# Two of seven Strassen products of an FFN tile done ahead for one chunk, in place of classically multiplied tiles

## The chip, the cores and the metric

The kernel runs on one core of one Trainium2 chip. A core has five engines that run side by side, each through its own instruction queue in order: TensorE (PE in the profile) multiplies, VectorE (DVE), ScalarE (ACT) and GpSimd (POOL) work on tiles elementwise, SyncE (SP) issues the DMAs. The metric is the device time of one execution in microseconds; lower is better. Before the change it is 2269.41 us, the median of three runs (2268.31 to 2272.55).

## The reference, cut to what matters

Two layer pairs over 1024 tokens of width 1024 in float32. Each pair is a mixer and a gated feed-forward network (FFN) with a causal depthwise convolution of width 3; the second mixer is itself a convolution of width 31. The change lies in the FFN's up-projection, which both pairs have:

```
def conv_ffn(h, w_up, dw_w, dw_b, w_down):          # h: 1024 x 1024, w_up: 1024 x 5632
    hh = causal_dwconv(h @ w_up, dw_w, dw_b)         # width 3 along the tokens
    a, gate = jnp.split(hh, 2, axis=-1)              # 2816 value and 2816 gate columns
    return (a * jax.nn.silu(gate)) @ w_down
x = x + conv_ffn(rms_norm(x, norm_ffn_g[l]), ...)
```

## The kernel before

Activations are held transposed (model dimension on the partitions). The tokens are two chunks of 512 (`CH`), the hidden width 22 tiles (`HT`) of 128 columns; hidden tile j has 128 gate columns and 128 value columns. Every float32 product is done in three fp32r passes (high x high, high x low, low x high), so each operand is kept as a high and a low part: ACT casts the high part (L143), DVE or GpSimd subtracts it for the low part (L147). One matmul is a 128x128 weight block by 128x512.

A **classical** hidden tile (`head_steps`) takes 48 matmuls a chunk and convolves straight out of PSUM on DVE (L585, L588). It needs no other chunk, so it can run while the second chunk is not ready: it fills PE beside the norm of the second chunk and the steps that build the combinations. Layer 0 has `PRE0` = 3 such tiles, layer 1 `PRE1` = 8.

All other tiles are **pair** tiles (`pair_steps`). The 2x2 block product {gate, value columns} x {two halves of the model dimension} x {two chunks} is done by seven products of 12 matmuls (84 in place of 96). Products 1 to 4 use the chunks' own activations (`hT[0]`, `hT[1]`), products 5 to 7 combinations of them (`T[1]`, `T[2]`, `T[3]`, the tiles t12 and t3), which `combos` builds once per layer (L636 to L639, transposed at L647, split at L649 and L650). The weights' sides are a1 = g1, a2 = g2, a4 = v2, a7 = g1 - v1, and a5, a6, a3, sums built one on the other at L700, L703 and L705. PSUM banks A and C accumulate: product 1, then 6, 7 and 4 into A, 5 and 3 into C, 2 into a bank of its own; between them ACT copies out what an output needs (L715, L718, L721, L732) and DVE adds (L723, L725, L728) into `row` tiles. Each row is then convolved in a two-bank PSUM tile, of which there is one: ACT starts it (L686), DVE adds two taps (L688), ACT takes SiLU of the gate (L730), DVE multiplies (L734).

In layer 1 the down-projection is done by seven products as well, over pairs of hidden tiles j and j + 11; `sums` (L554 to L558, three operations on GpSimd, one on DVE) forms their combinations after the second tile of a pair, called through `settle()` at the start of the next tile. The tile framework puts each engine's instructions in order from the program's order and its own costs; `interleave` mixes two lists of steps. A tile waits for a free buffer of its tag: 8 operand splits `hl`, 4 raw weight tiles, 4 rows, 4 single banks.

The lines that the prediction's steps touch: products L680, operand sums L700 to L705, low parts L147, adds L723 to L728, taps L688, and

```
a5 = part(s, "dve")
nc.vector.tensor_sub(out=s, in0=s, in1=g1)
a6 = part(s, "dve")
nc.gpsimd.tensor_sub(out=s, in0=g2, in1=s)
```

Of the kernel before, what the change touches and what calls it, by code (L numbers as in the profile page):

```python
# [58 lines left out]
def trunk_kernel(ctx: ExitStack, tc: tile.TileContext, x, norm_mix_g, norm_ffn_g, ab_w_in, ab_w_out,  # L59
# [515 lines left out]
    def head_steps(l, c, hT, js):  # L575

        dw, halo, w_up = dws[l], halos[l], ffn_w_up[l]

        def up(ct):
            ps = chan_mm(chan_unit(w_up, ct), hT[c])  # L580
            y = s2([P, CH])
            nc.scalar.activation(out=y, in_=ps, func=AF.Identity, scale=dw[:, 2, ct:ct + 1], bias=dw[:, 3, ct:ct + 1])  # L582
            for k in range(2):
                sh = 2 - k
                nc.vector.scalar_tensor_tensor(out=y[:, sh:], in0=ps[:, :CH - sh], scalar=dw[:, k, ct:ct + 1],  # L585
                                               in1=y[:, sh:], op0=ALU.mult, op1=ALU.add)
                if c > 0:
                    nc.vector.scalar_tensor_tensor(out=y[:, :sh], in0=halo[:, ct, k:2], scalar=dw[:, k, ct:ct + 1],  # L588
                                                   in1=y[:, :sh], op0=ALU.mult, op1=ALU.add)
            if c < NCH - 1:  # L590
                nc.vector.tensor_copy(out=halo[:, ct, :], in_=ps[:, CH - 2:])
            return y

        cur = {}

        def up_g(j):
            cur["g"] = yg = up(HT + j)
            nc.scalar.activation(out=yg, in_=yg, func=AF.Silu)

        def up_a(j):  # L600
            ya = up(j)
            nc.vector.tensor_tensor(out=ya, in0=ya, in1=cur["g"], op=ALU.mult)
            if l == 0:
                store_split(ya, s2([P, CH], F32R), j, slice(c * CH, (c + 1) * CH))
            elif c == 0:
                nc.sync.dma_start(out=phs[:, SLOT[1 + j // HH], j % HH, :], in_=ya)
            elif j < HH:
                cur["v"] = ya
            else:
                jj = j - HH  # L610
                old = s4([P, S])
                nc.sync.dma_start(out=old.rearrange("p (i c) -> p i c", i=2), in_=phs[:, 0:3:2, jj, :])
                sums(jj, old[:, :CH], cur["v"], old[:, CH:], ya)
                nc.sync.dma_start(out=phs[:, SLOT[4], jj, :], in_=ya)
                nc.sync.dma_start(out=phs[:, SLOT[7], jj, :], in_=cur["v"])

        return [f for j in js for f in (lambda j=j: up_g(j), lambda j=j: up_a(j))]
# [553 lines left out]
```

## Time and profile before

| | us |
|---|---|
| median of 3 runs | 2269.41 (2268.31 to 2272.55) |
| the profiled execution itself | 2265.38 |
| its span, first to last instruction | 2263.6 |
| PE busy | 2138.7 (94%) |
| DVE busy | 1481.1 (65%) |
| ACT busy | 1092.8 (48%) |
| POOL busy | 905.1 (40%) |
| mean granted TensorE clock | 0.972 of full speed |

In time, layer 0's classical tiles and combinations lie about 505 to 597 us, its pair tiles 597 to 958. The convolution mixer's end with layer 1's first classical tiles is at 1466 to 1640, the rest of them with norm and combinations at 1640 to 1755, layer 1's pair tiles at 1755 to 2030, its down-projection after that. An engine is listed as busy only while an instruction runs; idle time is listed in front of the instruction that ended it, with the engine and tile that released it.

### The profile page before, as it was taken

How to read it: one execution, taken by the hardware profiler on the slowest of the kernel's cores; microseconds unless marked ns; L12 is line 12 of the kernel's file. 1: busy time of each engine (PE TensorE's matmuls, PEld its weight loads, DVE VectorE, ACT ScalarE, POOL GpSimd, SP SyncE). 2: the span in 40 equal slices, each digit the busy share in tenths (PEclk: the TensorE clock that was granted, in tenths of full speed). 3: DMA queues.
4: the chain of work that ended last, by engine and by line, in shares of the span. 5: the costliest groups of instructions: out<-in, count | busy, mean ns of one | idle time of the engine just before them, and what ended most of it. 6: DMA issues, size and time to landing. Idle time of an engine off the chain costs nothing. (4 is left out here: it accounts for less than half of the span.)

```text
span 2263.6 us, 28251 instructions
## 1 busy us (share of the span) xinstructions
PE 2138.7 (94%) x9846; PEld 1755.1 (78%) x9846; DVE 1481.1 (65%) x2671; ACT 1092.8 (48%) x1899; POOL 905.1 (40%) x772
## 2 busy tenths in 40 slices
PE   8989999898999999999999979989998999999987
PEld 6768777787788888878788868767777888878876
DVE  5456787458666666600399569996576576756686
ACT  4245665244455555522455474555443454544354
POOL 1222010134344443344489827963544455530011
PEclk9999999999999999999999979989989999999999
DMA  6375433466233333588655723432653223238433
GB/s 226 112 244 172 128 124 134 141 231 197 75 112 105 108 107 109 201 305 286 212 168 168 259 60 100 152 100 93 221 165 127 95 91 117 93 132 319 130 98 107
DMA packets 300495, 346.58 MB, mean 153 GB/s; under 512 B 12988, under 2 KB 207296, under 8 KB 299840
## 3 DMA queue, kind: packets, MB, share of 16 engines
q1 hardware_dynamic: 300352, 344.77, 46.3%
q8 instruction: 78, 1.28, 0.2%
q14 instruction: 65, 0.53, 0.1%
HBM read 261.62 MB, written 83.10 MB: 152 GB/s over the span
## 5 line engine op out<-in xcount | busy, mean ns | idle before, releaser
L147 POOL TENSOR_TENSOR hl<-raw,hl 128x512 fp32r<-128x512 f32 x424 | 570.5, 1364 | 605.4 <-ACT hl L143 511.5
L307 PE MATMUL bank<-big,hl 128*128 128x512 f32 x1824 | 427.7, 394 | 4.1 <-ACT big L223 2.4
L270 PE MATMUL bank<-hl,big 128*128 128x512 f32 x1728 | 422.1, 400 | 7.2 <-ACT big L143 2.8
L143 ACT CAST hl<-raw 128x512 fp32r<-128x512 f32 x476 | 280.0, 618 | 257.5 <-issue 96.9
L307 PEld LDWEIGHTS bank<-big,hl 128*128 128x128 f32 x1824 | 343.2, 189 | 76.6 <-ACT big L223 3.3
L270 PEld LDWEIGHTS bank<-hl,big 128*128 128x128 f32 x1728 | 325.1, 192 | 78.1 <-ACT big L143 3.3
L680 PE MATMUL bank<-big,hl 128*128 128x512 f32 x1584 | 375.3, 390 | 0.3 <-ACT hl L143 0.3
L680 PEld LDWEIGHTS bank<-big,hl 128*128 128x128 f32 x1584 | 297.1, 188 | 64.0 <-ACT hl L143 1.0
L680 PE MATMUL bank<-t,hl 128*128 128x512 f32 x1188 | 290.4, 395 | 6.5 <-ACT hl L143 6.0
L688 DVE SCALAR_TENSOR_TENSOR bank<-row,dw,bank 128x1024 f32<-128x1024 f32 x132 | 169.7, 1286 | 162.8 <-ACT bank L686 161.6
L680 PEld LDWEIGHTS bank<-t,hl 128*128 128x128 f32 x1188 | 224.4, 189 | 57.6 <-ACT hl L143 6.9
L862 PE MATMUL bank<-hl,ph 128*128 128x512 f32 x1056 | 247.9, 395 | 5.3 <-DMA ph<-phd 3.3
L1006 DVE SCALAR_TENSOR_TENSOR sbank<-yb,cw,sbank 128x512 f32<-128x512 f32 x352 | 246.0, 749 | 5.0 <-ACT sbank L995 1.8
L862 PEld LDWEIGHTS bank<-hl,ph 128*128 128x128 f32 x1056 | 199.8, 190 | 49.7 <-DMA ph<-phd 4.3
L824 PE MATMUL bank<-hl 128*128 128x512 f32 x726 | 176.1, 397 | 10.4 <-DVE s L734 4.4
L824 PEld LDWEIGHTS bank<-hl 128*128 128x128 f32 x726 | 138.9, 192 | 42.1 <-ACT hl L143 5.0
L1003 POOL TENSOR_TENSOR ap<-ap,pr 128x512 f32<-128x512 f32 x112 | 147.8, 1319 | 14.2 <-ACT ap L998 10.3
L143 ACT CAST hl<-s 128x512 fp32r<-128x512 f32 x110 | 68.3, 621 | 108.8 <-POOL s L705 50.3
L1002 ACT ACTIVATE pr<-yb,cw 128x512 f32<-128x512 f32 x112 | 80.7, 723 | 63.5 <-POOL ap L1003 62.8
L705 POOL TENSOR_TENSOR s<-raw,s 128x512 f32<-128x512 f32 x33 | 43.6, 1320 | 157.9 <-DVE hl L147 83.5
L1112 POOL TENSOR_TENSOR xr<-xr,gain 128x512 f32<-128x512 f32 x10 | 14.5, 1481 | 201.5 <-ACT xn L1104 176.1
L585 DVE SCALAR_TENSOR_TENSOR s<-bank,dw,s 128x510 f32<-128x510 f32 x88 | 65.5, 745 | 35.8 <-ACT s L582 34.8
(202 smaller groups left out, 2577.3 us busy)
## 6 DMA issues: line engine op xcount, KB each, us to landing
raw<-in_ffn_w_up SPq DMA_DIRECT2D x110, 512.0 KB
ph<-phd SPq DMA_DIRECT2D x88, 512.0 KB
raw<-in_ffn_w_down SPq DMA_DIRECT2D x44, 512.0 KB
phd<-s SPq DMA_DIRECT2D x38, 512.0 KB
ph<-phs SPq DMA_DIRECT2D x33, 512.0 KB
raw<-in_conv_w_in SPq DMA_DIRECT2D x32, 512.0 KB
raw<-in_ab_w_in SPq DMA_DIRECT2D x32, 256.0 KB
qd<-s SPq DMA_DIRECT2D x32, 256.0 KB
```

What stands on the lines that cost most here:

```text
L143: nc.scalar.copy(out=hl_hi, in_=raw)
L147: eng.tensor_sub(out=hl_lo, in0=raw, in1=hl_hi.bitcast(F32))
L270: nc.tensor.matmul(ps, lhsT=hT[t // TPC][:, sa, d, tok(t)], rhs=units[d][:, sw, :], start=(n == 0), stop=(n == 3 * DT - 1))
L307: nc.tensor.matmul(ps, lhsT=hv[d // 4][:, sw, d % 4, :], rhs=hT[:, sa, d, :], start=(n == 0), stop=(n == 3 * DT - 1))
L585: nc.vector.scalar_tensor_tensor(out=y[:, sh:], in0=ps[:, :CH - sh], scalar=dw[:, k, ct:ct + 1], in1=y[:, sh:], op0=ALU.mult, op1=ALU.add)
L680: nc.tensor.matmul(ps, lhsT=hv[:, sw, d, :], rhs=B[n](sa, d), start=(start and i == 0), stop=(i == 11), skip_group_check=True)
L688: nc.vector.scalar_tensor_tensor(out=y, in0=r[:, k:k + S], scalar=dw[:, k, ct:ct + 1], in1=y, op0=ALU.mult, op1=ALU.add)
L824: nc.tensor.matmul(ps[k], lhsT=a[:, sa, k * P:(k + 1) * P], rhs=w[:, sw, :], start=(n in (5, 2, 1) and js[0] == 0 and i == 0), stop=(end a ...
L862: nc.tensor.matmul(ps, lhsT=phs[i][:, sa, k * P:(k + 1) * P], rhs=wds[i][:, sw, :], start=(dp == 0 and n == 0), stop=(dp == DP - 1 and n = ...
L1002: nc.scalar.activation(out=pr, in_=ys[ct][:, k:k + CH], func=AF.Copy, scale=cw[:, ct, k:k + 1])
L1003: nc.gpsimd.tensor_add(out=st["ap"], in0=st["ap"], in1=pr)
L1006: nc.vector.scalar_tensor_tensor(out=st["acc"], in0=ys[ct][:, k:k + CH], scalar=cw[:, ct, k:k + 1], in1=st["acc"], op0=ALU.mult, op1=ALU.add)
```

## The change

No tile is classical any more. `ahead_steps` does products 1 and 2 of chunk 0 alone (24 matmuls: a1 and a2 by `hT[0]`) for some hidden tiles. It keeps product 1 (ACT copy) and product 1 + product 2 (DVE add), the gate row's first half, and stores both to DRAM (`pcd`, 512 KB a tile). Later all 22 tiles are pair tiles. An **early** one loads these two, needs only 60 matmuls, and adds product 1 on DVE wherever before it was in bank A or copied by ACT: p5, u2 and the first half of the value row become DVE adds of a bank and `p1` in place of ACT copies, and the gate row's first half needs no operation. In layer 0 the 9 even tiles 0 to 16 are early (4 beside the norm of the second chunk, 5 beside the combinations), in layer 1 sixteen tiles, 0 to 15 (9, 3 and 4). Layer 1's pair tiles run in the order 0, 11, 1, 12, ..., so its first eleven are all early and the other eleven alternate. Per layer the matmuls are: ahead 288 to 216 and pairs 1596 to 1632 in layer 0, ahead 768 to 384 and pairs 1176 to 1464 in layer 1.

Besides: the low part of a6 goes from DVE to GpSimd; `settle()` moves from the tile's start behind the add of product 3; stores of y, phs and phd are put off until the next tile's loads are issued, and kept in that order; the SiLU output gets one buffer of its own; the classical convolution is gone.

```
-PRE0 = 3
-PRE1, PRE1_LATE = 8, 2
+AHEAD0, AHEAD1 = (4, 5), (9, 3, 4)
...
+    def ahead_steps(l, hT, js):
+        def f(j):
...
+            pc = s4([P, 2, CH])
+            a1, a2 = part(g[:, :512], "pool"), part(g[:, 512:], "pool")
+            A, B = bank(), bank()
+            product(A, a1, lambda sa, d: hT[0][:, sa, d, :], True, True)
+            nc.scalar.copy(out=pc[:, 0, :], in_=A)
+            product(B, a2, lambda sa, d: hT[0][:, sa, 4 + d, :], True, True)
+            nc.vector.tensor_add(out=pc[:, 1, :], in0=B, in1=pc[:, 0, :])
+            nc.sync.dma_start(out=pcd[:, j, :, :], in_=pc)
...
+            early = j in ahead
+            rg, rv_, p1 = row(), row(), up_pool.tile([P, CH], F32, tag="p1", name="p1", bufs=2)
+            if early:
+                nc.sync.dma_start(out=p1, in_=pcd[:, j, 0, :])
+                nc.sync.dma_start(out=rg[:, 2:2 + CH], in_=pcd[:, j, 1, :])
+            run(stores)
+            stores.clear()
             s = s2([P, 512])
-            a1 = part(g1, "pool")
+            if not early:
+                a1 = part(g1, "pool")
             nc.vector.tensor_add(out=s, in0=v1, in1=v2)
             a5 = part(s, "dve")
             nc.vector.tensor_sub(out=v1, in0=g1, in1=v1)
             nc.vector.tensor_sub(out=s, in0=s, in1=g1)
-            a6 = part(s, "dve")
+            a6 = part(s, "pool")
...
+            A, C = bank(), bank()
+            p5, u2 = s2([P, CH]), s2([P, CH])
+            if not early:
+                product(A, a1, B[1], True, False)
+                nc.scalar.copy(out=p1, in_=A)
+            product(C, a5, B[5], True, False)
+            if early:
+                nc.vector.tensor_add(out=p5, in0=C, in1=p1)
+            else:
+                nc.scalar.copy(out=p5, in_=C)
+            product(A, a6, B[6], early, False)
+            if early:
+                nc.vector.tensor_add(out=u2, in0=A, in1=p1)
+            else:
+                nc.scalar.copy(out=u2, in_=A)
+            product(C, a3, B[3], False, True)
+            nc.vector.tensor_add(out=rg[:, 2 + CH:], in0=C, in1=u2)
             settle()
...
+            product(A, a7, B[7], False, False)
             nc.vector.tensor_add(out=rv_[:, 2 + CH:], in0=A, in1=p5)
+            if not early:
+                Bk = bank()
+                product(Bk, a2, B[2], True, True)
+                nc.vector.tensor_add(out=rg[:, 2:2 + CH], in0=Bk, in1=p1)
-            yg = s4([P, S])
+            yg = up_pool.tile([P, S], F32, tag="yg", name="yg", bufs=1)
             nc.scalar.activation(out=yg, in_=conv(rg, HT + j), func=AF.Silu)
+            product(A, a4, B[4], False, True)
+            if early:
+                nc.vector.tensor_add(out=rv_[:, 2:2 + CH], in0=A, in1=p1)
+            else:
+                nc.scalar.copy(out=rv_[:, 2:2 + CH], in_=A)
...
-    interleave(head_steps(0, 0, hF0, order(0)[:PRE0]),
-               norm_steps(1, xtile, norm_ffn_g[0], hF0, spill=(xd[0], xnd)), 0.0, 0.4)
+    interleave(mid0, norm_steps(1, xtile, norm_ffn_g[0], hF0, hb=bank, spill=(xd[0], xnd)), 0.0, 0.8)
...
-            interleave(head_steps(l, 1, hT, js[:pre]), first, 0.0, 0.6)
-            run(last)
-            run(pair_steps(l, hT, T, js[pre:], up_pool))
+            interleave(late, first + last, 0.0, 1.0)
+            run(pair_steps(l, hT, T, order(l), ahead, up_pool))
```

PE's queue in layer 1's pair stage, before: from product 3 of one tile (bank_15344 and bank_15343 are its C and A, bank_15496 and bank_15497 the next tile's A and C; t12 and t3 are the combinations, big the chunks' own activations):

```order
L680 MATMUL bank_15344<-big_14091,hl_15327 128x512 x12
L680 MATMUL bank_15343<-t3_14373,hl_15330 128x512 x12
L680 MATMUL bank_15496<-big_12766,hl_15457 128x512 x9
L680 MATMUL bank_15497<-t12_14371,hl_15461 128x512 x12
L680 MATMUL bank_15343<-big_14091,hl_15336 128x512 x12
L680 MATMUL bank_15566<-big_12766,hl_15476 128x512 x12
```

The same place after the change, from product 3 of the third early tile (bank_14724 and bank_14723 are its C and A) into the fourth (bank_14846 and bank_14845):

```order
L584 MATMUL bank_14724<-big_13972,hl_14714 128x512 x12
L584 MATMUL bank_14723<-t3_14209,hl_14717 128x512 x12
L584 MATMUL bank_14723<-big_13972,hl_14720 128x512 x12
L584 MATMUL bank_14846<-t12_14207,hl_14827 128x512 x12
L584 MATMUL bank_14845<-t12_14208,hl_14832 128x512 x12
L584 MATMUL bank_14846<-big_13972,hl_14836 128x512 x12
```

Before, the next tile's product 1 and product 5 stand ahead of product 4; after, products 3, 7 and 4 of the one tile are followed at once by product 5 of the next, on hl_14827.

DVE's queue at that place before, from the last two taps of a tile's value row to the next tile's low parts (s2_15609 is the sum for its a5 and a6):

```order
L688 SCALAR_TENSOR_TENSOR bank2_15447<-row_15341,dw1_678,bank2_15447 128x1024 x2
L734 TENSOR_TENSOR s4_15446<-bank2_15447,s4_15427 128x1024
L558 TENSOR_TENSOR s2_15487<-s4_15446,sx_15483 128x512
L728 TENSOR_TENSOR row_15492<-bank_15566,s2_15510 128x512
L700 TENSOR_TENSOR s2_15609<-raw_15606 128x512
L702 TENSOR_TENSOR raw_15606<-raw_15605,raw_15606 128x512
L147 TENSOR_TENSOR hl_15614<-s2_15609,hl_15614 128x512
L703 TENSOR_TENSOR s2_15609<-s2_15609,raw_15605 128x512
L723 TENSOR_TENSOR row_15492<-bank_15497,s2_15538 128x512
L147 TENSOR_TENSOR hl_15619<-s2_15609,hl_15619 128x512
```

And after, from the add behind product 7 (bank_14723) of the third early tile to the adds behind products 5 and 6 of the fourth:

```order
L710 TENSOR_TENSOR row_14698<-bank_14723,s2_14725 128x512
L660 SCALAR_TENSOR_TENSOR bank2_14786<-row_14696,dw1_678,bank2_14786 128x1024 x2
L719 TENSOR_TENSOR row_14698<-bank_14723,p1_14700 128x512
L558 TENSOR_TENSOR s2_14770<-s4_14686,sx_14766 128x512
L680 TENSOR_TENSOR s2_14825<-raw_14811 128x512
L682 TENSOR_TENSOR raw_14811<-raw_14810,raw_14811 128x512
L660 SCALAR_TENSOR_TENSOR bank2_14805<-row_14698,dw1_678,bank2_14805 128x1024
L146 TENSOR_TENSOR hl_14827<-s2_14825,hl_14827 128x512
L660 SCALAR_TENSOR_TENSOR bank2_14805<-row_14698,dw1_678,bank2_14805 128x1024
L683 TENSOR_TENSOR s2_14825<-s2_14825,raw_14810 128x512
L723 TENSOR_TENSOR s4_14804<-bank2_14805,yg_14785 128x1024
```

The low part hl_14827, which product 5 of the fourth tile needs, stands five operations behind the add (L719) that reads bank_14723 after product 4; the low part for product 6 has left this queue.

The alternating tiles of layer 1, after, on PE: from product 7 of an early tile (bank_16189) to product 5 of the ordinary one (bank_16316), whose product 1 is bank_16315's:

```order
L584 MATMUL bank_16189<-t3_14209,hl_16183 128x512 x12
L584 MATMUL bank_16315<-big_12780,hl_16290 128x512
L584 MATMUL bank_16189<-big_13972,hl_16186 128x512 x12
L584 MATMUL bank_16316<-t12_14207,hl_16294 128x512 x12
```

Here eleven of the twelve matmuls of product 1 stand ahead of these rows, and product 5 follows product 4 directly.

## Rows read from the trace of the kernel before

**Rows 1.** The page's busy time, share of the span and instructions of each engine.
```profile
PE 2138.7 (94%) x9846; PEld 1755.1 (78%) x9846; DVE 1481.1 (65%) x2671; ACT 1092.8 (48%) x1899; POOL 905.1 (40%) x772
```

**Rows 2.** Busy by stage: window, us; PE, PEld, DVE, ACT, POOL; PE clock, DMA.
```profile
700.00:796.00 96.00, 96.00 (x422) 78.98 (x421) 60.73 (x71) 53.00 (x76) 38.69 (x40) 1.00 0.33 110
...
1466.00:1490.00 24.00, 8.99 (x39) 7.17 (x38) 23.43 (x30) 13.11 (x19) 15.32 (x11) 0.57 0.38 128
1490.00:1640.00 150.00, 144.54 (x658) 117.94 (x656) 101.81 (x202) 80.29 (x139) 79.36 (x61) 0.98 0.42 137
1640.00:1755.00 115.00, 102.94 (x472) 85.86 (x473) 81.48 (x118) 44.06 (x72) 52.14 (x42) 0.93 0.47 150
...
1832.00:1908.00 76.00, 76.00 (x335) 62.51 (x334) 54.94 (x54) 37.62 (x57) 41.47 (x39) 1.00 0.32 104
```

**Rows 3.** The chain of waits: start us, length us, what.
```profile
1754.57 265.67 PE bank L680 x1152
2020.24 2.72 PE sbank L824 x12
```

**Rows 4.** PE's waits, 1466 to 2040: us in total, times, longest us.
```profile
PE bank L220 <- DVE big L224: 15.1, 4, 5.2
PE bank L680 <- ACT hl L143: 6.0, 1, 6.0
```

**Rows 5.** DVE by line, 1640 to 1755: busy us, mean ns, idle before.
```profile
L585 DVE SCALAR_TENSOR_TENSOR s<-bank,dw,s 128x511 f32<-128x511 f32 x18 | 13.4, 747 | 0.5
L585 DVE SCALAR_TENSOR_TENSOR s<-bank,dw,s 128x510 f32<-128x510 f32 x18 | 13.4, 744 | 17.7 <-ACT s L582 17.6
L588 DVE SCALAR_TENSOR_TENSOR s<-halo,dw,s 128x2 f32<-128x2 f32 x16 | 11.9, 743 | 0.0
L588 DVE SCALAR_TENSOR_TENSOR s<-halo,dw,s 128x1 f32<-128x1 f32 x16 | 9.3, 581 | 0.0
```

**Rows 6.** DVE by line in layer 0's pair tiles, 700 to 892.
```profile
L147 DVE TENSOR_TENSOR hl<-s,hl 128x512 fp32r<-128x512 f32 x20 | 13.6, 682 | 0.0
```

**Rows 7.** DVE by line in layer 1's pair tiles, 1775 to 1985.
```profile
L688 DVE SCALAR_TENSOR_TENSOR bank<-row,dw,bank 128x1024 f32<-128x1024 f32 x44 | 56.6, 1286 | 35.5 <-ACT bank L686 35.2
L147 DVE TENSOR_TENSOR hl<-s,hl 128x512 fp32r<-128x512 f32 x22 | 20.2, 920 | 4.7 <-ACT hl L143 4.3
L734 DVE TENSOR_TENSOR s<-bank,s 128x1024 f32<-128x1024 f32 x11 | 13.4, 1221 | 0.3
L700 DVE TENSOR_TENSOR s<-raw 128x512 f32<-128x512 f32 x11 | 12.7, 1153 | 0.0
L702 DVE TENSOR_TENSOR raw<-raw 128x512 f32<-128x512 f32 x11 | 12.5, 1134 | 0.3
L703 DVE TENSOR_TENSOR s<-s,raw 128x512 f32<-128x512 f32 x11 | 12.5, 1132 | 0.3
L723 DVE TENSOR_TENSOR row<-bank,s 128x512 f32<-128x512 f32 x11 | 7.5, 684 | 1.0 <-PE bank L680 1.0
...
L558 DVE TENSOR_TENSOR s<-s,sx 128x512 f32<-128x512 f32 x5 | 3.5, 692 | 20.1 <-POOL sx L556 20.1
```

**Rows 8.** ACT's cast of an operand sum, 1775 to 1985.
```profile
L143 ACT CAST hl<-s 128x512 fp32r<-128x512 f32 x33 | 20.5, 622 | 32.2 <-DVE s L703 21.5 <-POOL s L705 10.6
```

**Rows 9.** GpSimd by line, 1775 to 1985.
```profile
L147 POOL TENSOR_TENSOR hl<-s,hl 128x512 fp32r<-128x512 f32 x11 | 14.3, 1300 | 8.0 <-ACT hl L143 8.0
L705 POOL TENSOR_TENSOR s<-raw,s 128x512 f32<-128x512 f32 x11 | 14.3, 1296 | 43.8 <-DVE hl L147 43.8
```

**Rows 10.** Timeline of DVE and GpSimd, 1846 to 1862: start us, us, engine, instruction.
```profile
1852.85 0.68 DVE L725 TENSOR_TENSOR row<-bank,s 128x512 f32<-128x512 f32 x1
...
1854.63 1.70 DVE L700 TENSOR_TENSOR s<-raw 128x512 f32<-128x512 f32 x1
...
1853.24 1.30 POOL L147 TENSOR_TENSOR hl<-s,hl 128x512 fp32r<-128x512 f32 x1 [0.73 <-ACT hl L143]
1854.50 4.69 POOL L147 TENSOR_TENSOR hl<-raw,hl 128x512 fp32r<-128x512 f32 x3
```

More of the change, by code (lines that the diff above doesn't have):

```diff
@@ L573, in settle @@
             pending.pop(0)()
[L575 to L617, printed above, removed]
@@ new lines, in part, with product @@
+    def part(raw, lo_eng):
+        hl = whl.tile([P, 2, 512], F32R, tag="whl", name="hl")
+        split_hi_lo(raw, hl[:, 0, :], hl[:, 1, :], lo_eng=lo_eng)
+        return hl.rearrange("p s (d c) -> p s d c", c=P)
+    def product(ps, hv, rhs, start, stop):
+        i = 0
+        for d in range(4):
+            for sw, sa in PASSES:
+                nc.tensor.matmul(ps, lhsT=hv[:, sw, d, :], rhs=rhs(sa, d), start=(start and i == 0),
+                                 stop=(stop and i == 11), skip_group_check=True)
+                i += 1
@@ L669, in row @@
             return r
-        def part(raw, lo_eng):
-            hl = whl.tile([P, 2, 512], F32R, tag="whl", name="hl")
-            split_hi_lo(raw, hl[:, 0, :], hl[:, 1, :], lo_eng=lo_eng)
-            return hl.rearrange("p s (d c) -> p s d c", c=P)
-        def product(ps, n, hv, start, stop):
-            i = 0
-            for d in range(4):
-                for sw, sa in PASSES:
-                    nc.tensor.matmul(ps, lhsT=hv[:, sw, d, :], rhs=B[n](sa, d), start=(start and i == 0),
-                                     stop=(i == 11), skip_group_check=True)
-                    i += 1
         def conv(r, ct):
@@ L707, in f @@
             a7 = part(v1, "pool")
[L708 removed]
+            if not early:
+                a2 = part(g2, "pool")
             a4 = part(v2, "pool")
[L710 to L719 removed]
@@ L954, in trunk_kernel, with ffn_rest, ahead_of @@
     open_psum(1)
-    interleave(head_steps(0, 0, hF0, order(0)[:PRE0]),
-               norm_steps(1, xtile, norm_ffn_g[0], hF0, spill=(xd[0], xnd)), 0.0, 0.4)
-    def ffn_rest(l, hT, pre):
+    def ffn_rest(l, hT, ahead, late):
         with tc.tile_pool(name=f"up{l}", bufs=1) as up_pool:
             first, last, T = combos(l, hT, up_pool)
-            js = order(l)
-            interleave(head_steps(l, 1, hT, js[:pre]), first, 0.0, 0.6)
-            run(last)
-            run(pair_steps(l, hT, T, js[pre:], up_pool))
-    ffn_rest(0, hF0, PRE0)
+            interleave(late, first + last, 0.0, 1.0)
+            run(pair_steps(l, hT, T, order(l), ahead, up_pool))
+    def ahead_of(l, hT, counts):
+        js = [2 * k for k in range(counts[0] + counts[1])] if l == 0 else order(1)[::2] + order(1)[1::2]
+        js = js[:sum(counts)]
+        steps = ahead_steps(l, hT, js)
+        parts = [steps[sum(counts[:i]):sum(counts[:i + 1])] for i in range(len(counts))]
+        return set(js), parts
+    a0, (mid0, late0) = ahead_of(0, hF0, AHEAD0)
+    interleave(mid0, norm_steps(1, xtile, norm_ffn_g[0], hF0, hb=bank, spill=(xd[0], xnd)), 0.0, 0.8)
+    ffn_rest(0, hF0, a0, late0)
+    run(stores)
+    stores.clear()
     C = ExitStack()
@@ L1127, in trunk_kernel @@
         settle()
+        run(stores)
         run(ds[2:4])
```

59 lines of the change are left out of this document (23 added, 36 removed).

## The prediction

> **What bounds the kernel now.** I read the page's busy times first: PE is busy 94% of the span, DVE 65% [rows 1]. That is a mean, so next came the busy time by stage [rows 2]. In the pair tiles of layer 0 PE is busy 96.00 of 96.00 us for five hidden tiles and DVE 60.73; in layer 1 PE 76.00 of 76.00 us for four, DVE 54.94. Stages ahead of layer 1's pair tiles have gaps: 15.0 us in 1466-1490, 5.5 us in 1490-1640, 12.1 us in 1640-1755. The chain of waits then shows the whole pair stage of layer 1 as one unbroken PE piece, 265.67 us for 1152 recorded matmuls, and a clean dozen of 128x512 matmuls at 2.72 us, so 0.2267 us each [rows 3]. The waits of PE from 1466 to 2040 are 15.1 us on the block that DVE turns behind the convolution's taps (L224) and single ones of 4 to 6 us at stage borders [rows 4]. So in the pair tiles before, matmul count is time, and DVE has 28 to 37% to spare.
>
> **What goes.** 132 matmuls: 36 in layer 0 (72 fewer ahead of the pairs, 36 more in them), 96 in layer 1 (384 fewer ahead, 288 more in the pairs). 132 x 0.2267 = **29.9 us**, if PE stays the bound: 8.2 in layer 0, 21.8 in layer 1. The classical tiles' own DVE work goes too; in 1640-1755 the four forms of L585 and L588 take 48.0 of DVE's 81.48 us [rows 2, 5]. That matters only where PE waits for it.
>
> **What stays.** PE's 15.1 us on L224 hang on taps and a queue order that the change leaves alone: nothing. At the two borders into the pair stages the change takes cover away (layer 1: 480 classical matmuls become 168) and takes DVE work away with it. In 1640-1755 that leaves 168 x 0.2267 = 38 us of matmuls and the transposes over a chain of norm and combination tiles whose DVE part is at most 38 us (81.48 - 48.0 + seven new adds of 0.68). I take no change in the gaps there, with ends of -6 us (half of the 12.1 us goes) and +8 us (two more waits of the size of L680's 6.0 and L224's mean of 3.8, less 2 that overlap).
>
> **Layer 0's pair stage.** Early and ordinary tiles alternate. Two tiles cost PE 60 + 84 matmuls, 32.6 us. DVE had 12.1 us a tile (60.73/5); it loses one low part a tile (0.68 us, [rows 6]), and an early tile gains two PSUM adds net (p5, u2 and the value row's first half come, the gate row's first half goes) of 0.68 each, as L723 [rows 7]: 24.2 - 1.4 + 1.4 = 24.2 of 32.6 us. Following both queues through one period with these durations, each DVE result that PE waits for is there at least 2.8 us early, and the next ordinary tile's product 1, which needs no DVE work, stands where a wait could open. Nothing, with an upper end of 5 us.
>
> **Layer 1's first eleven pair tiles: all early.** Here I expect the loss. PE needs 60 x 0.2267 = 13.6 us a tile, 27.2 for two. DVE's 29 instructions for two tiles are 8 taps x 1.286, 2 gates x 1.221, 10 PSUM adds x 0.68, 6 operand sums at 1.13 to 1.15, 2 low parts x 0.92 and one L558 x 0.69 [rows 7]: 10.3 + 2.4 + 6.8 + 6.8 + 1.8 + 0.7 = 28.9 us. So even without one idle moment DVE takes 1.7 us more than PE. And it can't run without idling, as the order shows: after the 3rd, 5th, 7th and 9th early tile PE goes from product 4 of one tile straight to product 5 of the next on a low part that DVE makes only behind the add that waits for that product 4. Between them on DVE stand that add 0.68, L558 0.69, the sum 1.15, the difference 1.13, a tap 1.29 and the low part 0.92: 5.9 us, of which two matmuls that need only the high part cover 0.45. PE waits 5.4 us; with the uncontended 0.68 us for the three SBUF operations it would be 4.3.
> Behind it comes the low part now on GpSimd: tap 1.29, difference 1.13, cast 0.62 [rows 8], low part 1.30 [rows 9] are 4.3 us, and PE has 12 matmuls, 2.7 us, to do meanwhile: 1.6 us more. Product 3 needs another GpSimd sum 1.30, cast 0.62 and low part 1.30 against 2.7 us: 0.5. Together 7.5 us at each of four places, 30. After the 11th tile an ordinary one follows whose product 1 covers 2.7 of 5.4: 2.7. I take **33 us**. The lower end is the one wait at its uncontended length, 4 x 4.3 = 17; the upper end a period of 36.9 us, which comes out when I follow DVE's queue through two tiles with the contended means (the second tile's product 4 then also waits 1.6 us for the add behind product 7): 4 x 9.7 + 4 = 43.
>
> **Layer 1's other eleven pair tiles** alternate, but with DVE at the contended durations. PE goes from an early tile's product 4 to the next tile's product 5 again, with only the add 0.68 and the low part 0.92 between, less 0.45, and from product 7 to product 4 with one matmul against an add: 0.68 - 0.23. That is 1.6 us, five times: **8 us**, between 0 (DVE ahead) and 12.
>
> **GpSimd.** In the trace an SBUF sum of DVE (L700) takes 1.70 us beside GpSimd's low parts, which run back to back (4.69 us for three), while a PSUM add just before, beside GpSimd's low part too, takes 0.68 [rows 10]. The new adds (PSUM and p1) are of the second kind, and I price them at 0.68. The Trainium skill, SBUF — State Buffer, "Who interferes with whom", says that a DVE instruction with two SBUF inputs and a GpSimd instruction that reads SBUF lock each other out for a whole instruction, and that one with a single SBUF input is spared; the trace agrees with 1.70 against 0.68. By that rule the low part moved to GpSimd speaks against the change: it saves DVE 0.68 to 0.92 us a tile and can hold up another operation for up to 1.0 us.
>
> **Sum.** -29.9 + 33 + 8 = +11 us on the profiled run's 2265.38 us (span 2263.6): 2276.5. The median of the runs is 4.0 us above that run, so **2280 us**. With all ends: -29.9 + 17 + 0 - 6 = -19 to -29.9 + 43 + 12 + 5 + 8 = +38, 2250 to 2307.
>
> **Rivals.**
> 1. *PE stays the bound everywhere* (chance 0.13): DVE's SBUF operations in layer 1 fall to layer 0's 0.68 us, since ordinary tiles' low parts 1 and 2 no longer run on GpSimd there, and DVE reaches the sums before product 4 ends. For it: GpSimd has five operations an early tile where it had six. Against: the order fixes the add ahead of the sums. The time is 2269.4 - 29.9 = 2239.5, or 2250 with the four waits at half.
> 2. *The stages ahead of layer 1's pairs give back more than matmuls* (0.18), the one case that puts a real DVE loss on the faster side. Their gaps are 32.5 us [rows 2]; they have lost the classical tiles' convolution on DVE. If DVE finishes taps, norm and combinations early enough to halve the gaps, -16 stands against +11: 2264; with the four waits uncontended too (-13): 2251. It decides from a gap gain of about 16 us on. Against: 15.1 of the 32.5 are the L224 wait, whose queue is the same.
> 3. *A draw* (0.19): the four waits at 4.3 us with the rest of that place covered (17 + 3), and 8 behind: -2 us, 2267, and up to 2274.
> 4. *GpSimd's lock costs more than its mean* (0.06, on the slower side): every one of the 9 SBUF operations of two tiles at 1.70 instead of 1.13, 5 us for each of eleven half-pairs and alternating pairs near the bound: up to +25 on the forecast, 2300.
> That the change does not do what it says is no case: the matmul count falls as stated.
>
> **How the numbers follow.** The forecast has 0.44, with 2274 to 2295 as its own range. About 0.2% (4.5 us) is what a measurement of this kernel can tell from no change. Faster by more than that, below 2265: rival 1 and most of rival 2, 0.30. Within: the draw and the edges of its neighbours, 0.20. Slower: 0.50. The range 2246 to 2297 leaves out most of rival 1 and the last of rival 4.
>
> **What would show it.** Layer 1's pair stage should have a PE gap of 4 to 7 us about every 35 us in its first eleven tiles, released by DVE's or ACT's operand work for product 5, and DVE busy above 80% there; small gaps after; layer 0's pair stage none to speak of; about 33 us for two of the first tiles if I am too gloomy, 27 if rival 1 holds. I am wrong if PE is 98% busy in those tiles, or if the stages from 1466 to 1755 shrink by much more than the 480 - 168 and 72 matmuls that leave them.

## The result and the profile after

The changed kernel takes **2294.73 us** (median of 4 runs, 2288.95 to 2297.5) against 2268.86 us (4 runs, 2262.27 to 2272.55) for the kernel before on the same chip: a ratio of **1.0114, 95% interval [1.0083, 1.0145]**. It is slower, as forecast, and inside the range, but further out than the 2280 us of the likeliest case. The profiled execution took 2294.10 us (span 2292.2), 28.7 us more than the one of before; the medians differ by 25.9 us. The ledger below is of the two profiled executions.

The page's busy line, which answers to [rows 1]:

```profile
PE 2129.5 (93%) x9714; PEld 1727.9 (75%) x9714; DVE 1517.8 (66%) x2670; ACT 1063.8 (46%) x1825; POOL 938.2 (41%) x816
```

PE has exactly 132 instructions fewer, so the matmuls did go, but its busy time fell only 9.2 us, where 132 x 0.2267 is 29.9, and the span grew. I cut both spans at the same landmarks and set each piece against its matmul count:

| piece, from landmark to landmark | before, us | after, us | difference | by count alone |
|---|---|---|---|---|
| layer 0's up-projection, 505 to its last pair product | 452.7 | 452.2 | -0.5 | -8.2 |
| from there to layer 1's first early work | 530.0 | 528.3 | -1.7 | 0 |
| layer 1, ahead of the pair tiles | 256.7 | 170.9 | -85.8 | -87.1 |
| layer 1, pair tiles | 278.1 | 392.2 | +114.1 | +65.3 |
| rest | 240.8 | 243.3 | +2.5 | 0 |

Two pieces don't follow the count: layer 1's pair tiles (48.8 us over it) and layer 0 (7.7 us over it).

**Layer 1's pair tiles.** Windows of the changed kernel (length; busy PE, PEld, DVE, ACT, POOL; PE clock, DMA share, GB/s): the eleven early tiles behind the last transposes, two periods of two early tiles within them, and two alternating tiles.

```profile
1668.74:1852.14 183.40, 157.00 (x639) 122.49 (x637) 134.53 (x152) 67.36 (x87) 88.20 (x88) 0.94 0.41 128
1706.68:1741.95 35.27, 30.06 (x121) 23.33 (x121) 26.23 (x30) 12.43 (x16) 17.34 (x17) 0.95 0.45 142
1778.89:1815.75 36.86, 30.35 (x120) 23.38 (x120) 26.28 (x30) 12.42 (x16) 17.32 (x17) 0.92 0.43 135
1886.28:1921.70 35.42, 34.16 (x144) 26.57 (x144) 26.16 (x28) 15.83 (x23) 20.72 (x19) 1.00 0.40 127
```

Read the first line against [rows 2], where PE was busy 76.00 of 76.00 us: 636 of its matmuls are pair products, 144.2 us at 0.2267. PE needs 183.4, that is 39.2 more: 26.4 idle and 12.8 in which it is busy but slower, at a granted clock of 0.94. DVE, at 134.5 of 183.4 us (73%), is not full. The last line shows the alternating tiles: 144 matmuls are 32.6 us, the period is 35.4 at clock 1.00. The waits of PE in the eleven tiles (us in all, times, longest) are 26.3 of the 26.4 us, and none of them is for a DMA; the stage before had one, the 6.0 us of [rows 4] near its start:

```profile
PE bank L584 <- ACT hl L142: 19.8, 5, 5.3
PE bank L584 <- DVE row L710: 4.5, 4, 1.4
PE bank L584 <- DVE hl L146: 1.4, 4, 0.7
PE bank L584 <- POOL hl L146: 0.6, 2, 0.4
```

One such place in PE's timeline, and what DVE and ACT do in it. L710 is the add behind product 7, L719 the new add behind product 4, L660 a tap, L658 the convolution's start on ACT, L680 and L682 the next tile's operand sum and difference, L142 the cast of the sum, L146 its low part:

```profile
1807.52 2.98 PE L584 MATMUL bank<-big,hl 128*128 128x512 f32 x12 [0.88 <-DVE row L710]
1815.75 1.22 PE L584 MATMUL bank<-t,hl 128*128 128x512 f32 x2 [5.25 <-ACT hl L142]
```

```profile
1809.78 1.29 DVE L660 SCALAR_TENSOR_TENSOR bank<-row,dw,bank 128x1024 f32<-128x1024 f32 x1 [1.28 <-ACT bank L658]
1810.98 0.68 DVE L719 TENSOR_TENSOR row<-bank,p 128x512 f32<-128x512 f32 x1
1811.58 1.28 DVE L660 SCALAR_TENSOR_TENSOR bank<-row,dw,bank 128x1024 f32<-128x1024 f32 x1
1812.77 0.69 DVE L558 TENSOR_TENSOR s<-s,sx 128x512 f32<-128x512 f32 x1
1813.37 0.69 DVE L680 TENSOR_TENSOR s<-raw 128x512 f32<-128x512 f32 x1
...
1812.89 1.02 ACT L716 ACTIVATE yg<-bank 128x1024 f32<-128x1024 f32 x1 [3.15 <-DVE bank L660]
1813.95 1.21 ACT L658 ACTIVATE bank<-row,dw 128x1024 f32<-128x1024 f32 x1
1815.10 0.60 ACT L142 CAST hl<-s 128x512 fp32r<-128x512 f32 x1
```

PE ends product 4 at 1810.50 and next needs product 5's operand. DVE only gets to the operand's sum at 1813.37, behind the add, two taps and L558; ACT could cast it at 1814.06, but is still in the SiLU and the start that waited for the same taps, and casts at 1815.10. After the wait PE is also slower: the granted clock is 0.50 (the level of 1.2 GHz) for 4.5 us, and 0.99 (nearly all at 2.4 GHz) from 1821.00 to the end of the eleven tiles:

```profile
1815.75:1820.20 4.45, 4.29 (x9) 2.99 (x10) 4.26 (x5) 0.62 (x1) 0.64 (x2) 0.50 0.87 335
1821.00:1852.14 31.14, 27.98 (x122) 22.37 (x120) 21.68 (x25) 12.87 (x17) 17.23 (x16) 0.99 0.30 86
```

The chain of waits (start, length, what), where [rows 3] had one PE piece of 265.67 us, runs through these queues and leaves PE out for ten microseconds. On DVE it begins with L723, the multiply of the tile before, which frees the one two-bank tile that ACT's start (L658) needs; then it goes through the taps, the SiLU and the next start to the low part:

```profile
1803.83 2.83 PE bank L584 x12
...
1807.29 1.23 DVE s L723
...
1808.54 1.22 ACT bank L658
...
1809.78 1.29 DVE bank L660
...
1817.13 1.22 PE bank L584 x2
```

**Layer 0.** Its steady pair tiles did stay full: 96.00 of 96.00 us, DVE at 72.66 where [rows 2] has 60.73. The loss is earlier, beside chunk 1's norm and the combinations. Each block has the window and two of PE's waits (us in all, times, longest), on the norm (L220, after L211) and on the combinations (L647, after L632). The first is the kernel before:

```profile
505.00:597.00 92.00, 84.53 (x402) 69.18 (x403) 75.50 (x130) 43.36 (x73) 31.80 (x26) 0.96 0.49 158
PE bank L220 <- DVE big L224: 5.5, 2, 3.7
PE sbank L647 <- DVE big L650: 1.0, 1, 1.0
```

```profile
700.00:796.00 96.00, 96.00 (x422) 78.86 (x421) 72.66 (x84) 50.19 (x68) 45.84 (x48) 1.00 0.43 142
505.00:597.00 92.00, 80.34 (x370) 65.19 (x371) 54.46 (x97) 33.82 (x62) 29.45 (x26) 0.93 0.53 175
PE bank L211 <- DVE xn L195: 5.7, 1, 5.7
PE sbank L632 <- DVE t L635: 4.4, 4, 2.1
```

With 32 instructions fewer in 92 us, PE has 4.2 us more of idle time. The waits on the norm were as long before; those on the combinations grew. Up to the combinations' first transpose there are 148 big matmuls, before 144. Beside the combinations there are 40 fewer, 9.1 us by count, and that stretch is only 2.5 us shorter (43.5 for 46.0). Over layer 0's whole piece PE is idle 5.0 us longer, and its busy time falls by 5.5 where the count says 8.2: of the 7.7 us, 5.0 are waiting and 2.7 slower work.

### The profile page after: what moved, and what is told of

Its sections match the earlier page's. It is cut to its first block, busy times and chain, and to the rows that moved or that the text cites. A ratio compares the mean times of both kernels' runs of the same rounds, so it can differ in the third digit from the quotient of the medians.

```text
span 2292.2 us, 28159 instructions
## 1 busy us (share of the span) xinstructions
PE 2129.5 (93%) x9714; PEld 1727.9 (75%) x9714; DVE 1517.8 (66%) x2670; ACT 1063.8 (46%) x1825; POOL 938.2 (41%) x816
## 4 chain that ended last, share of the span: by engine, by line
PE 68%; DVE 12%; issue 6%; DMA 6%; ACT 5%; POOL 3%; SPq 0%; ACTq 0%; POOLq 0%; DVEq 0%
PE bank L584 31%; PE bank L269 14%; PE bank L306 8%; PE bank L814 5%; PE bank L852 4%; POOL hl L146 3%; PE sbank L814 2%; DVE bank L660 1%; DVE hl L146 1%; ACT hl L142 1%; DVE y L180 1%; DMA s<-xnd 1%; ACT e L445 1%; DMA ph<-phd 1%; DMA kd<-sec 1%
## 5 line engine op out<-in xcount | busy, mean ns | idle before, releaser
L146 POOL TENSOR_TENSOR hl<-raw,hl 128x512 fp32r<-128x512 f32 x380 | 507.0, 1355 | 531.5 <-ACT hl L142 444.5
L584 PE MATMUL bank<-big,hl 128*128 128x512 f32 x2112 | 514.3, 395 | 11.3 <-DVE row L710 7.3
L584 PEld LDWEIGHTS bank<-big,hl 128*128 128x128 f32 x2112 | 397.4, 190 | 103.6 <-issue 6.2
L584 PE MATMUL bank<-t,hl 128*128 128x512 f32 x1584 | 399.0, 402 | 24.8 <-ACT hl L142 19.8
L584 PEld LDWEIGHTS bank<-t,hl 128*128 128x128 f32 x1584 | 302.3, 193 | 102.0 <-ACT hl L142 24.2
L142 ACT CAST hl<-raw 128x512 fp32r<-128x512 f32 x432 | 252.5, 619 | 240.5 <-issue 94.9
L660 DVE SCALAR_TENSOR_TENSOR bank<-row,dw,bank 128x1024 f32<-128x1024 f32 x176 | 226.3, 1286 | 84.9 <-ACT bank L658 81.3
L146 POOL TENSOR_TENSOR hl<-s,hl 128x512 fp32r<-128x512 f32 x88 | 120.6, 1370 | 169.5 <-ACT hl L142 165.9
L306 PE MATMUL bank<-big,hl 128*128 128x512 f32 x768 | 176.7, 390 | 0.8 <-ACT big L214 0.7
L142 ACT CAST hl<-s 128x512 fp32r<-128x512 f32 x143 | 88.5, 619 | 188.6 <-DVE s L683 81.7
L306 PEld LDWEIGHTS bank<-big,hl 128*128 128x128 f32 x768 | 144.1, 188 | 31.1 <-ACT big L214 1.2
L814 PEld LDWEIGHTS bank<-hl 128*128 128x128 f32 x726 | 137.5, 190 | 39.2 <-issue 4.9
L658 ACT ACTIVATE bank<-row,dw 128x1024 f32<-128x1024 f32 x88 | 106.5, 1210 | 102.6 <-DVE s L723 43.9
```

Source lines behind the costliest of these rows:

```text
L142: nc.scalar.copy(out=hl_hi, in_=raw)
L146: eng.tensor_sub(out=hl_lo, in0=raw, in1=hl_hi.bitcast(F32))
L306: nc.tensor.matmul(ps, lhsT=hv[d // 4][:, sw, d % 4, :], rhs=hT[:, sa, d, :], start=(n == 0), stop=(n == 3 * DT - 1))
L584: nc.tensor.matmul(ps, lhsT=hv[:, sw, d, :], rhs=rhs(sa, d), start=(start and i == 0), stop=(stop and i == 11), skip_group_check=True)
L658: nc.scalar.activation(out=y, in_=r[:, 2:], func=AF.Identity, scale=dw[:, 2, ct:ct + 1], bias=dw[:, 3, ct:ct + 1])
L660: nc.vector.scalar_tensor_tensor(out=y, in0=r[:, k:k + S], scalar=dw[:, k, ct:ct + 1], in1=y, op0=ALU.mult, op1=ALU.add)
```

## The experiments

Twelve kernels were run. Ratios are to the kernel before on the same chip; the change itself has 1.0114 [1.0083, 1.0145].

**1. Alternate in layer 1 too.** Eleven early tiles instead of sixteen, each beside an ordinary one.
```
-AHEAD0, AHEAD1 = (4, 5), (9, 3, 4)
+AHEAD0, AHEAD1 = (4, 5), (6, 2, 3)
```


> Layer 1 does products 1 and 2 ahead for only the 11 tiles that stand first in a pair (6, 2 and 3 of them in the three stages), so that early and ordinary tiles alternate through all of its pair stage, as in layer 0. The matmul count is unchanged (24 + 60 = 84). Theory (back-to-back early tiles make PE wait for DVE's operands): the pair stage takes 11 x 35.4 us = 390 us, as now 391, although it has 120 matmuls more, and the stages ahead lose these 120 matmuls, 27 us; total near 2268, -20 to -30 us against the changed kernel. Rival (each early tile costs PE the same extra wherever it stands, 44.7 us over 16 tiles, 2.8 us each): -14 us, near 2281. Second rival (the stages ahead are held by the norm and combination chain and don't shrink): no gain, 2290 or more.


Measured: 2284.01 us, 1.0070 [1.0054, 1.0087]. No place with 5 us is left; every period is as the alternating ones of the change. The pair stage takes 390.0 us with 120 more matmuls (27.2 us) than the change's 392.2. But the stage ahead shrinks to 154.9 us, 16.0 less, not 27; new waits open there. The first line is its window, then PE's waits in it:

```profile
1488.50:1643.39 154.89, 133.13 (x596) 106.08 (x597) 100.95 (x194) 73.81 (x129) 66.78 (x50) 0.91 0.47 155
```
```profile
1530.23 0.47 PE L1029 MATMUL bank<-ident,yb 128*128 128x128 f32 x1 [5.13 <-DVE yb L1006]
1535.30 1.12 PE L1044 MATMUL sbank<-ident,yn 128*128 128x128 f32 x4 [4.60 <-ACT yn L1038]
```
It follows that early tiles in a row cost about 29 us here (392.2 + 27.2 - 390.0), and that early matmuls were also the cover of other chains, here the mixer's convolution (yb) and the norm behind it (yn). Of the 11.2 us that the stage ahead does not give, 7.2 are more idle time of PE; the rest is slower work, at a clock of 0.91 for 0.96. The pair stage went as the theory had it, the stage ahead in part as the rival on cover. The total is near the first rival's 2281, but 2.8 us for each early tile would leave the pair stage at 405 us.

**2. The low part back on DVE.**
```
-            a6 = part(s, "pool")
+            a6 = part(s, "dve")
```


> Only the low part of a6 goes back from GpSimd to DVE. Theory (the order of DVE's queue sets the wait): PE's 5.25 us wait for the cast of the next tile's a5 stays, product 6 gets its low part some 0.6 us earlier, DVE has 0.69 us more a tile; between -6 and +6 us against the changed kernel. Rival (GpSimd's extra operation locks DVE's sums and is what made it slow): -15 us or more.


Measured: 2287.57 us, 1.0088 [1.0071, 1.0105]; the interval overlaps the change's, so the total alone would not settle it. The trace does, by an accident of the schedule: two early tiles now come in two orders. Windows of one period of each, and their waits on PE:

```profile
1705.23:1742.14 36.91, 30.62 (x120) 23.84 (x121) 26.75 (x32) 12.56 (x16) 14.77 (x15) 0.91 0.43 135
1779.33:1810.85 31.52, 28.53 (x120) 22.21 (x121) 27.06 (x32) 12.48 (x16) 14.72 (x16) 1.00 0.51 159
```
```profile
1713.46 0.79 PE L584 MATMUL bank<-t,hl 128*128 128x512 f32 x1 [5.25 <-ACT hl L142]
1783.66 0.73 PE L584 MATMUL bank<-t,hl 128*128 128x512 f32 x2 [1.35 <-ACT hl L142]
```
DVE's queue in the first period and in the second, up to the sum for the next product 5 (L680):
```profile
1704.39 0.69 DVE L710 TENSOR_TENSOR row<-bank,s 128x512 f32<-128x512 f32 x1 [0.42 <-PE bank L584]
1705.00 1.22 DVE L723 TENSOR_TENSOR s<-bank,yg 128x1024 f32<-128x1024 f32 x1
1707.49 1.29 DVE L660 SCALAR_TENSOR_TENSOR bank<-row,dw,bank 128x1024 f32<-128x1024 f32 x1 [1.28 <-ACT bank L658]
1708.69 0.69 DVE L719 TENSOR_TENSOR row<-bank,p 128x512 f32<-128x512 f32 x1
...
1711.08 0.69 DVE L680 TENSOR_TENSOR s<-raw 128x512 f32<-128x512 f32 x1
```
```profile
1776.31 1.22 DVE L723 TENSOR_TENSOR s<-bank,yg 128x1024 f32<-128x1024 f32 x1
1778.49 0.69 DVE L710 TENSOR_TENSOR row<-bank,s 128x512 f32<-128x512 f32 x1 [0.96 <-PE bank L584]
1779.10 2.61 DVE L660 SCALAR_TENSOR_TENSOR bank<-row,dw,bank 128x1024 f32<-128x1024 f32 x2
...
1782.21 0.69 DVE L680 TENSOR_TENSOR s<-raw 128x512 f32<-128x512 f32 x1
1782.81 0.69 DVE L719 TENSOR_TENSOR row<-bank,p 128x512 f32<-128x512 f32 x1
```
The same matmuls, as much DVE work (26.8 and 27.1 us), and 5.4 us between them; PE waits 5.25 us in the first and 1.35 in the second. The order differs in two places. In the second period the multiply L723 stands ahead of the add that waits for product 7 (L710), so ACT can start the next convolution earlier; and the add that waits for product 4 (L719) stands behind the sum, not between the taps. Counted from the start of product 4 (1705.23 and 1779.33), the first tap comes at 2.26 and -0.23 us and the sum at 5.85 and 2.88: about 2.5 of the 3.0 us go with L723's place, and 0.6 with L719's. Neither swap was run by itself. The order in the queue decides, not the amount of work. 2.1 of the 5.4 us are the same 120 matmuls at clock 0.91 and 1.00.

**3. Stores issued where they arise, not behind the next tile's loads.**
```
-    pin = tc.keep_in_program_order
+    pin = lambda i: i
   ...
-    pending, stores = [], []
+    class Now(list):
+        def append(self, f):
+            f()
+    pending, stores = [], Now()
```


> The stores of y, phs and phd are issued where their data is made, as before the change, not put off until after the next tile's loads. Theory: the pair stages stay as they are, and only the start of layer 1's down-projection, which is 6.6 us longer than before the change, gets shorter: -4 to -7 us against the changed kernel. Rival (deferred stores do no harm, or stores at once delay weight loads): 0 to +5 us.


Measured: 2297.03 us, 1.0138 [1.0113, 1.0164]. Nothing is gained, so the theory is wrong; the layer-1 wait is again 19.8 us in five. The 6.6 us that it set out to explain came of a wrong landmark; that piece is the +2.5 of the ledger.

**4. The next tile's operands written ahead of product 4.**
```
+            n = js.index(j) + 1
+            if n < len(js):
+                nxt.append(prep(js[n]))   # loads, sums and parts 5, 6, held in this order on DVE
             yg = up_pool.tile([P, S], F32, tag="yg", name="yg", bufs=1)
   ...
```
Left out here is `prep`, which takes a tile's loads, its sums and its parts up to the sixth out of the tile's own steps, those of GpSimd too.


> The next tile's operand sums for products 5 and 6 and the low part of a5 are written ahead of product 4 of the tile before and kept on DVE's queue ahead of the add that waits for product 4; nothing is added or left out. Theory (order, not amount of DVE work): PE's waits of 3.1 to 5.3 us between product 4 and the next product 5 in the first eleven tiles of layer 1 go, two of those tiles take 29 to 32 us instead of 36.9, the pair stage loses 15 to 28 us: 2267 to 2280. Rival (DVE's amount of work is the bound, 26 us busy of every 36 us and its waits for ACT's first tap): the wait turns up at another product and less than 8 us is gained.


Measured: 2350.95 us, 1.0374 [1.0353, 1.0396], much worse. The 5 us waits are gone (the longest on the cast is 2.7 us), and small ones stand in many tiles instead. Waits of PE from 1640 to 2100 (L719 is there the add behind product 7, L712 the one behind product 6):

```profile
PE bank L584 <- DVE row L719: 16.5, 10, 1.7
PE bank L584 <- POOL hl L146: 13.1, 21, 0.6
PE bank L584 <- DVE s L712: 7.1, 15, 0.5
```
Two early tiles still take 35.1 us, and layer 0's pair tiles, full before, fall to 90.03 of 96.00 us. DVE is busy 23.7 of the 35.1 us: again not its amount of work. But the edit also moves the next tile's casts and GpSimd's parts ahead, and 13.1 us of the waits are on GpSimd's low parts; what each part of it cost is not shown.

**5. The kernel before with that low part on GpSimd**, nothing else.
```
-            a6 = part(s, "dve")
+            a6 = part(s, "pool")
```


> The kernel before with one part of the change alone: the low part of a6 goes from DVE to GpSimd. Theory: PE is busy all through the pair stages of the kernel before and DVE has a quarter to spare, so nothing moves, within 5 us of the kernel before. Rival (GpSimd's extra operation costs by itself, through DVE's locked-out sums): 5 to 15 us slower.


Measured: 2267.21 us, 1.0002 [0.9991, 1.0013] over 10 runs. By itself this part of the change costs nothing, in a kernel whose PE does not wait for it.

**6. Experiments 1 and 2 together.**


> Both edits that helped together: early and ordinary tiles alternate in layer 1, and the low part of a6 is on DVE again. Theory (two separate gains): the 10.7 us of the first and some of the 7.2 us of the second, 2277 to 2281 against 2284 for the first alone. Rival (both took the same waits of the first eleven tiles): no gain over the first, 2283 to 2287.


Measured: 2280.22 us, 1.0068 [1.0051, 1.0086]. In us the gain over the change is 14.5, where the two had 10.7 and 7.2; by ratio it can't be told from experiment 1. With no two early tiles in a row there is hardly a place left for the low part to matter, which would explain it.

**7. Layer 0's norm of chunk 1 ordered as before.**
```
-  norm_steps(1, xtile, norm_ffn_g[0], hF0, hb=bank, spill=(xd[0], xnd)), 0.0, 0.8)
+  norm_steps(1, xtile, norm_ffn_g[0], hF0, spill=(xd[0], xnd)), 0.0, 0.4)
```


> In layer 0 the norm of the second chunk turns its tiles through the two-bank PSUM tile and is mixed in at 0.4 again, as before the change; all else is the changed kernel. Layer 0's stage from 505 us to its last pair product became only 0.6 us shorter, with 8.2 us of matmuls gone; a wait of 5.7 us for the norm's second tile is new there. Theory (the norm chain with too little to do beside it, however it is written): the wait moves, within 4 us of the changed kernel. Rival (the half banks or the mixing place are the cause): -4 to -8 us.


Measured: 2292.23 us, 1.0120 [1.0095, 1.0146]: not to be told from the change. In its profiled execution, the fastest of its four, layer 0's piece takes 446.7 us, 5.5 less than in the change. PE has no wait on the norm left there, and 8.1 us on the combinations in place of 4.4; the longest:

```profile
559.02 1.97 PE L632 MATMUL sbank<-ident,s 128*128 128x128 f32 x8 [6.83 <-DVE t L635]
```
The profiles of the five kernels whose layer 0 is the change's (the change, experiments 1, 8, 9 and 11) have 449.9 to 452.2 us for that piece. Experiments 10 and 12, which share this edit and the low part on DVE, have 444.7 and 445.0, experiment 6, which has only the latter, 449.3. So some 3 to 5.5 us of layer 0 go with the norm's order, which the total does not resolve.

**8. One tap less** for both rows in layer 1's first eleven pair tiles.
```
+            taps = (1,) if l == 1 and j in js[:11] else (1, 0)
```


> Leaves out the second of the two DVE taps of both rows in the first eleven pair tiles of layer 1 (so the convolution lacks its oldest token there): 2.6 us of DVE work a tile less, matmuls and other engines unchanged. Theory (PE waits through DVE's queue between product 4 and the next product 5, on which two of these taps stand): the period of two early tiles falls from 36.9 us to 29 to 33 us, and the longest wait from 5.3 to under 3 us. Rival (the wait is set by ACT's casts and starts of taps, or by GpSimd): the period stays above 35 us.


`conv` then runs over `taps`; that line is left out here. Measured once: 2285.38 us. The waits on ACT's cast fall to 10.7 us in 4, the longest from 5.3 to 2.7; a period only to 34.7 to 35.3. Waits of PE in the pair stage, and a period's window:

```profile
PE bank L584 <- ACT hl L142: 10.7, 4, 2.7
PE bank L584 <- DVE hl L146: 7.6, 10, 1.1
```
```profile
1776.34:1811.02 34.68, 30.03 (x121) 23.36 (x121) 21.26 (x26) 12.60 (x16) 17.32 (x17) 0.95 0.46 144
```
So the taps do stand in the way, as the theory had it; but 5 us of DVE work taken out of a period shorten it by 2, and the next links of the same handshake come forward, as the rival had it.

**9. The settling of finished pairs** (`settle()`, which issues the sums around L558) back ahead of the products.
```
-            settle()
             product(A, a7, B[7], False, False)
   ...
+            settle()
             A, C = bank(), bank()
```


> Only settle() goes back to where it stood before the change, ahead of a tile's products, so that L558 and its GpSimd sums are due earlier. The order then has the next tile's products 5 and 6 ahead of product 4 in the first eleven tiles too, and the next tile's operand sums ahead of the add behind product 4 on DVE, with the same work on every engine. Theory (order decides): PE's 3 to 5 us waits for the next a5 go; L558, which waits up to 4 us for GpSimd's sums, now stands ahead of the adds behind products 5 and 6 and brings a shorter wait once in two tiles. The period of two early tiles is 31 to 34 us in place of 36.9, that of two alternating tiles 33 to 34 in place of 35.4: -15 to -30 us against the changed kernel, 2265 to 2280. Rival (L558's wait for GpSimd takes the place of the one removed): within 6 us of the changed kernel.


Measured: 2345.27 us, 1.0349 [1.0320, 1.0379]: the theory is badly wrong. DVE's L558 waits for GpSimd, and behind it now stands the new add (L699 there) that must empty product 5's bank before PE may go on. Waits of PE from 1640 to 2100, then DVE's queue:

```profile
PE bank L584 <- DVE s L699: 81.6, 10, 11.2
```
```profile
1826.18 0.69 DVE L558 TENSOR_TENSOR s<-s,sx 128x512 f32<-128x512 f32 x1 [3.94 <-POOL sx L556]
1826.79 0.68 DVE L699 TENSOR_TENSOR s<-bank,p 128x512 f32<-128x512 f32 x1
```
In the kernel before the copy of that bank was ACT's, and L558 could wait on DVE ahead of the products. This also shows why settling had to move in this change.

**10. Experiments 6, 7 and 9 together.**


> The four edits together: early and ordinary tiles alternate in layer 1, the low part of a6 is on DVE, layer 0's norm is as before the change, settle() stands first. Theory (the edits act in different places): 2280 for the first two, 5 us less in layer 0, and the eleven alternating pairs of layer 1 at 33 to 34 us instead of 35.2, 13 to 24 us: 2251 to 2262, faster than the kernel before. Rival (L558's wait for GpSimd's sums keeps the alternating pairs at 35 us): 2272 to 2277, slower than before.


Measured: 2343.40 us, 1.0338 [1.0306, 1.0370], by the same wait, 67.5 us in ten.

**11. L558 on GpSimd.**
```
-        nc.vector.tensor_sub(out=s4_, in0=a12, in1=s2_)
+        nc.gpsimd.tensor_sub(out=s4_, in0=a12, in1=s2_)
```


> Only L558, DVE's one operation of the combinations for the down-projection, goes to GpSimd behind the three that it waits for there; nothing else is changed. Theory (what stands on DVE's queue between product 4 and the next a5 sets the wait): 0.7 us less per two tiles on that queue, and DVE no longer waits for GpSimd in it; the alternating tiles get the low part of a5 ahead of the add behind product 4, and lose their 0.62 us wait. -5 to -14 us against the changed kernel. Rival (GpSimd's next low parts come 1.3 us later once in two tiles and PE waits for them): +0 to +6 us.


Measured: 2297.12 us, 1.0148 [1.0127, 1.0169]. The longest wait on the cast falls from 5.3 to 4.6 us, and waits on GpSimd's low parts rise from 0.6 to 3.1 us: no gain, as the rival had it.

**12. Experiments 1, 2, 7 and 11 together.**


> What helped, together: early and ordinary tiles alternate in layer 1, a6's low part on DVE, layer 0's norm as before the change, L558 on GpSimd; settle() stays where the change put it. Theory: 2280 for the first two, less 3 to 5 us in layer 0, less 0.6 to 1.5 us for each of eleven pairs of tiles in layer 1: 2258 to 2270, level with the kernel before or up to 0.4% faster. Rival (layer 0's gain and the sum's move don't add up with the rest): 2272 to 2280.


Measured: 2277.85 us, 1.0061 [1.0041, 1.0082]. It has the lowest median of the changed kernel's versions (by ratio not to be told from experiments 1 and 6), and is still slower than the kernel before; its alternating tiles take 35.6 us for 32.6 of matmuls. No version beat the kernel before.

## Why the prediction was right, and where its numbers were not

- **Direction and place: right.** The eleven early tiles of layer 1 lose more than the saved matmuls give, because PE goes from product 4 to the next tile's product 5 through DVE's in-order queue. Experiments 1 (no such neighbours: 29 us back in the pair stage), 2 (the same work in another order: 31.5 against 36.9 us) and 8 (one tap less: a longest wait of 2.7 for 5.3 us, and 2 us off the period) show it.
- **That place's price: 33 us forecast, 39.2 measured, of other parts.** The wait for product 5 was put at 24.3 us in five places and is 19.8; it ends with ACT's cast and not with DVE's low part, since ACT's queue stands behind the same taps. The operand work at the place shown took 0.69 us an operation and not 1.13 to 1.15; its means from 1706.68 to 1852.14 are 1.02 us (L680), 1.18 (L682), 0.68 (L683) and 0.82 (L146). GpSimd's low part, put at 1.6 us four times, cost 0.6 in all. What I had not priced in the likeliest case is 4.5 us of PE's waits for the add behind product 7 (it stood only in the upper end), and 12.8 us in which PE is busy but over its count. Against experiment 2's period at clock 1.00 (28.53 us for 120 matmuls), the two shown in the result (30.06 and 30.35 us for 120 or 121 at 0.95 and 0.92) lose 1.5 to 1.8 us, so over half of the 12.8 goes with the lower clock; the rest is there at 1.00 too.
- **DVE's load: wrong.** I expected it above 80% there; it is 73%. "Even without one idle moment DVE takes 1.7 us more than PE" did not decide: experiment 2 ran such a period in 31.5 us with 27.1 of DVE. The low part moved to GpSimd is no loss of its own (experiment 5). The Trainium skill, SBUF — State Buffer, "Who interferes with whom", has a DVE instruction with two SBUF inputs and a GpSimd instruction that reads SBUF lock each other out, which spoke against this edit, and spares one with a single SBUF input. The new adds, of the kind that it spares, took 0.69 us in these tiles, so the trace agrees there; that the moved low part costs time is shown by no run.
- **The alternating tiles: mis-sized.** Their stage, 1886.28 to 2048.90, is about 15 us over its 650 matmuls, 2.7 of it 12 matmuls of the down-projection mixed in; 8 was forecast. The waits are the two named, on the add behind product 7 (0.55 us) and the low part (0.62 us); they are 1.2 of the 2.8 us by which a period is over its count, and what the rest is stays open. The tile before, run at clock 0.91 after the last early one, is 4.0 us over its count, and I had nothing for it.
- **The step that failed: "Layer 0's pair stage. ... Nothing."** Its steady tiles stayed full, but the piece gave back 0.5 of 8.2 us. The prediction named both borders into the pair stages and worked out only layer 1's. There "I take no change in the gaps" held: 85.8 of 87.1 us came. In layer 0 the combinations lost 40 matmuls of cover and took 2.5 us less where the count is 9.1. Experiment 1 shows the same kind of loss in layer 1 once 120 more matmuls are taken out. The new order of layer 0's norm, which the prediction did not price, has a share too: 3 to 5.5 us by the profiles with and without it (experiment 7), though no total confirms it. How the 7.7 us divide between the two is not shown.
- **The sum.** In the ledger: -29.9 by count, +48.8 in layer 1's pairs (41 forecast), +7.7 in layer 0 (0), and about 2 in the rest (0). +11 became +28.7. These are differences from the kernel before, whose own pair stage in layer 1 was 14.3 us over its count; the 39.2, 4.0 and 15 us above are over the count alone.
- **The rivals.** PE is not the bound everywhere; the gaps gave nothing back; no draw. GpSimd's lock, the rival on the slower side, is not the reason though the time is near its 2300: the operations on SBUF did not rise to 1.70 us, their means are the 0.68 to 1.18 above.

Open: what the chip would do with a queue of DVE written out by hand in the order of experiment 2's good period, L723 ahead of L710 and the sum ahead of L719, for every early tile, and whether that would beat the kernel before. It was not tried.

## What to carry to other kernels

A copy from an accumulating bank on an idle engine cost nothing here, but the same step as an add on a busy in-order engine put that engine's whole queue into PE's path; before counting the saved matmuls, write down what stands between the result that PE waits for and the last thing that it gave. Price a wait with the slower stretch behind it, and look up what the removed matmuls had been covering, in every stage that they leave. When PE stalls on an engine that is not full, try its order before its load.

## What was unexpected of the hardware

After PE's wait of 5.25 us the granted clock was 0.50, the level of 1.2 GHz, for 4.5 us, and then close to 1.00, that of 2.4 GHz. After the wait of 3.08 us it was 0.50 from 1708.20 to 1710.00, 0.65 in the 2 us behind, then 1.00. Around waits of 1.35 us (experiment 2) and of 0.55 and 0.62 us (the alternating tiles) it stayed at 1.00. Over a period of two early tiles that gives means of 0.91 to 0.95: 120 matmuls took 30.6 us in experiment 2's period with the 5.25 us wait (0.91), and 28.5 us in the period with 1.35 us (1.00). So a wait of 5.25 us cost some 7 us, itself and 2.1 us of slower matmuls.
